# mLSTM's gates computed beside RWKV's first inverse, small gates in one pass, the early branch over two PSUM banks

## The chip, the cores and the metric

The kernel runs on one core of a Trainium2 chip. The core has a matrix engine (TensorE, PE), a vector engine (VectorE, DVE), a scalar engine (ScalarE, ACT), a general engine (GpSimd, POOL) and SyncE (SP), whose queue issues nearly all of the DMAs of this kernel. [...] The metric is device time in microseconds, the median of several executions; lower is better.

## The reference

Four layers over 512 tokens (256 context, 256 latent), 1024 channels. Each layer:

```python
hx = modulate(rmsnorm(x, norm1_g[l]), mod_x[0], mod_x[1])      # and hc for the context
gdn_x, rwkv_x, mlstm_x, gate_x = split_cols(hx @ w_in[l], col_groups)
a = gdn_branch(...); b = rwkv_branch(...); m = mlstm_branch(...)   # two directions each
merged = sum(sigmoid(gates[i]) * (branches[i] @ w_branch[i]) for i in range(3))
x = x + mod_x[2] * (merged @ w_out[l])
x = x + mod_x[5] * moe_ec(modulate(rmsnorm(x, norm2_g[l]), ...), ...)
```

The change touches the gates of mLSTM. Its scan keeps a running maximum per head and direction, from an input gate and the cumulated log of a forget gate:

```python
b = cumsum(log_sigmoid(fg + f_bias));  m_t = maximum(b_t + m, max_j(b_t - b_j + ig_j))
P = qk * exp(D - m_t);  num = exp(b + m - m_t) * (q @ C) + P @ v;  C = dec * C + wk.T @ v
```

These two gates of four heads and two directions, with gdn's eight decays and eight write strengths, come from 32 small columns of `w_in` ("small gates").

## The kernel before

Activations lie transposed, channels on partitions and the 512 tokens along the free axis, so a product with a block of 128 output channels fills one PSUM bank. Large products are exact to nearly fp32 by a split of both sides into a high and a low half of the one-pass type `fp32r`: three products for each 128 channels of depth (`dense`, L399 to L418). `load_w` (L387) loads raw weights four blocks of depth at a time into a buffer with the tag "raw" + f, casts them into "hi" + f on ScalarE and subtracts into "lo" + f on GpSimd (`split`, L383 to L385). f is "m" or "f"; each of these tags has two buffers, and the product goes to the bank "d" + f, of which there is one each ("dm", "df").

The kernel is written as streams of work. A planner orders each engine's instructions by a priority, a due time that the streams set with `at(t)` or `due(t, pace)` in units that are meant as microseconds of the layer; it gives buffers of one tag to the tiles that ask for them. Before a layer's clock starts at 0, `hh` and `hl`, the halves of the normed and modulated input, are made (L569 to L578). Then run, beside each other:
- `small_gates` (L653): 32 columns of small gates, as 16 fp32 matmuls in four column groups of 32 (two depths times `hh`, `hl`), copied, transposed and added up from four parts; softplus and the like follow, and `gdec`, `beta`, `igt` (input gate of mLSTM), `spf` (softplus of its forget gate).
- RWKV (streams "ai", "ac"): eight heads as four pairs. `rwkv_inputs` makes the inputs of a pair with `w_in` products of form "m", due from 40 us for pair 1; `rwkv_units` prepares two units in the tiles "AR" (three buffers), "BK" (one) and "t1" (five); `rwkv_pair` inverts triangular blocks (`tri_inverse`, L426: a substitution in 28 short VectorE steps between two trips through DRAM, then products; its tile `Zt` has the tag "BK") and runs the steps of the scan.
- gdn (stream "bi"): four heads, `w_in` products also of form "m", due from 95 us for head 1. In the program, gdn's heads 0 and 1 stand ahead of RWKV's pair 1.
- the fillers (L580 to L593): 36 `w_in` products of form "f" for the branch gates and mLSTM's q, k, v, spread over the layer, each copied out of "df" by ScalarE and stored in DRAM (`gates`). In the last layer they need only the latent half.
- mLSTM (L1279), due from 650, in the space that RWKV leaves: it loads q, k, v, transposes v and k, and then computes the gates: two padded tiles of gate columns, 16 matmuls for a transposed copy and a cumulated sum, three scans for the running maximum (L1342 to L1344), three exponentials, 16 transposes back to tokens into `tkm`, one product for the decays `dec`; the maximum goes to DRAM (`Md`) and comes back broadcast over partitions. The masked exponentials per head (L1399 to L1403), products and states follow.
- `first_branch` (L517), at 800: RWKV's output times `w_branch`, eight blocks of 128 channels. For each, `gated` (L510) loads the branch gate into `th`, multiplies (12 matmuls, bank "df"), forms (1 + th) times the product in VectorE (L515), and the result is stored in `part`. `th` has the tag "rawm".
- `second_branch` (L531), at 1500, loads gdn's output through tiles "him" and "lom" and splits it; `other_branches` (L539) does mLSTM's and gdn's products for the eight blocks, forms "f" and "m", and adds `part`. Then `w_out` and the expert mixture, which the change doesn't touch.

## Time and profile before

| | us |
|---|---|
| median of 3 runs | 4950.55 (4945.63 to 4950.76) |
| profiled execution | 4935.1 |
| its span, first to last instruction | 4933.3 |
| TensorE busy | 4447.4 (90%), 31792 matmuls |
| VectorE busy | 2927.6 (59%) |
| ScalarE, GpSimd busy | 1526.7 (31%), 1416.8 (29%) |
| granted TensorE clock, mean share of full speed | 0.954 |

The span holds four layers, which begin at about 43, 1303, 2553 and 3807 us; the last is shorter, since it needs only the latent tokens. The page gives sums over the whole span; what one stage waits for is read from views of a stretch: a table of busy times by stretch, the timeline, the waits of one engine or of the DMA queue, and the groups of instructions by line.

### The profile page before, as it was taken

Reading aid. Unit: us, or ns where it says so; the run is one execution under the profiler, and the core shown is the slowest. Engines: PE = TensorE matmul, PEld = TensorE weight load, DVE = VectorE, ACT = ScalarE, POOL = GpSimd, SP = SyncE. Lnnn points to the kernel's source line nnn. Section 1 sums busy time; section 2 is a strip of 40 time slices with the busy share of each in tenths; the row PEclk is TensorE's granted clock in tenths of the full one; section 3 lists DMA queues with packets and bytes.
Section 4 is the critical chain, followed back from the end, with each engine's and each line's share of the span. In section 5 each row is a group of like instructions: output and inputs, shape, how many; then the busy total and the mean of one; then the engine's idle time right before and its main releaser. Section 6 shows DMA issues by size and latency. Waiting matters only on the chain. (4 is left out here: it accounts for less than half of the span.)

```text
span 4933.3 us, 84704 instructions
## 1 busy us (share of the span) xinstructions
PE 4447.4 (90%) x31792; PEld 2903.0 (59%) x31792; DVE 2927.6 (59%) x8016; ACT 1526.7 (31%) x3100; POOL 1416.8 (29%) x1826
## 2 busy tenths in 40 slices
PE   7999999999889999989988999998998898887798
PEld 4666666653466666665336666666633666766532
DVE  4786767532477776663247777756423777767312
ACT  4343323221333332323124333332312433322211
POOL 3332323420243232242024323233301433332400
PEclk9999999999999999999999999999999899988899
DMA  6433446679632434457973244345698223333698
GB/s 228 118 111 109 123 150 202 230 268 386 238 105 66 124 113 125 152 190 265 386 282 112 66 115 118 111 146 167 243 382 300 88 78 85 88 87 108 222 386 310
DMA packets 716777, 886.01 MB, mean 180 GB/s; under 512 B 337072, under 2 KB 361264, under 8 KB 703568
## 3 DMA queue, kind: packets, MB, share of 16 engines
q1 hardware_dynamic: 716368, 880.60, 54.0%
q8 instruction: 251, 4.11, 0.3%
q14 instruction: 158, 1.29, 0.1%
HBM read 795.81 MB, written 84.63 MB: 178 GB/s over the span
## 5 line engine op out<-in xcount | busy, mean ns | idle before, releaser
L385 POOL TENSOR_TENSOR wlo<-wraw,whi 128x512 fp32r<-128x512 f32 x696 | 938.1, 1352 | 1725.8 <-ACT whi L384 1493.8
L411 PE MATMUL df<-big,whi 128*128 128x512 f32 (+1 forms) x2944 | 884.8, 382 | 0.0
L411 PE MATMUL dm<-big,whi 128*128 128x512 f32 (+1 forms) x2368 | 735.3, 390 | 0.0
L411 PE MATMUL df<-big,wlo 128*128 128x512 f32 (+1 forms) x1536 | 645.9, 420 | 65.9 <-ACT gt L590 21.4
L384 ACT CAST whi<-wraw 128x512 fp32r<-128x512 f32 x696 | 426.1, 617 | 886.3 <-PE df L411 446.8
L411 PEld LDWEIGHTS df<-big,whi 128*128 128x128 f32 x2944 | 562.4, 199 | 89.8 <-issue 3.8
L411 PE MATMUL dm<-big,wlo 128*128 128x512 f32 (+1 forms) x1248 | 524.8, 421 | 60.2 <-POOL wlo L385 17.4
L411 PEld LDWEIGHTS dm<-big,whi 128*128 128x128 f32 x2368 | 456.3, 197 | 80.1 <-issue 1.6
L411 PEld LDWEIGHTS df<-big,wlo 128*128 128x128 f32 x1536 | 303.9, 198 | 188.1 <-issue 102.0
L411 PEld LDWEIGHTS dm<-big,wlo 128*128 128x128 f32 x1248 | 245.5, 197 | 163.3 <-issue 57.6
L1686 PE MATMUL df<-mw,big 128*64 128x512 f32 x1024 | 282.8, 604 | 3.7 <-DMA mw<-in_w_dram 3.6
L1062 DVE SCALAR_TENSOR_TENSOR cv<-cv,par,cv 128x255 f32<-128x255 f32 (+3 forms) x472 | 253.8, 548 | 46.5 <-ACT cv L1059 42.6
L1686 PE MATMUL dm<-mw,big 128*64 128x512 f32 x1024 | 259.3, 596 | 5.6 <-DMA mw<-in_w_dram 5.6
L747 DVE SCALAR_TENSOR_TENSOR big<-cv,muc,big 128x252 f32<-128x252 f32 (+2 forms) x280 | 162.3, 603 | 40.8 <-ACT big L744 39.5
L1728 DVE SCALAR_TENSOR_TENSOR t<-t,df 128x512 f32<-128x512 f32 x32 | 22.0, 687 | 274.1 <-ACT t L1727 274.1
L1686 PEld LDWEIGHTS dm<-mw,big 128*64 128x64 f32 x1024 | 81.0, 137 | 164.5 <-issue 128.2
L385 POOL TENSOR_TENSOR mlof<-mrawm,mhif 128x512 fp32r<-128x512 f32 x9 | 11.6, 1284 | 540.3 <-ACT mhif L384 540.3
L212 PE MATMUL ai<-AR,BK 64*128 64x128 f32 (+1 forms) x1024 | 119.2, 313 | 44.8 <-POOL BK L930 21.7
L1745 PE MATMUL bi<-mw,mrawf 128*64 128x512 f32 x512 | 154.5, 601 | 0.3 <-DMA mw<-in_w_dram 0.3
L1686 PEld LDWEIGHTS df<-mw,big 128*64 128x64 f32 x1024 | 73.3, 136 | 131.4 <-issue 96.1
L1730 DVE TENSOR_TENSOR t<-t,dm 128x512 f32<-128x512 f32 x32 | 22.0, 687 | 193.6 <-PE dm L1686 193.6
L212 PEld LDWEIGHTS ai<-AR,BK 64*128 64x128 f32 x1024 | 91.2, 201 | 72.3 <-issue 30.3
(557 smaller groups left out, 7936.0 us busy)
## 6 DMA issues: line engine op xcount, KB each, us to landing
mw<-in_w_dram SPq DMA_DIRECT2D x768, 512.0 KB, 10.8
wraw<-in_w_in_dram SPq DMA_DIRECT2D x536, 256.0 KB, 2.8
adaw<-in_ada_w_dram SPq DMA_DIRECT2D x96, 1024.0 KB, 5.2
gates<-gt SPq DMA_DIRECT2D x114, 256.0 KB, 2.7
wraw<-in_w_branch_dram SPq DMA_DIRECT2D x96, 256.0 KB, 2.8
t<-gates SPq DMA_DIRECT2D x85, 256.0 KB, 4.3
TU<-zoai SPq DMA_DIRECT2D x128, 128.0 KB, 3.8
wraw<-in_w_out_dram SPq DMA_DIRECT2D x64, 256.0 KB, 4.2
```

The costliest lines, as they stand in the source:

```text
L212: mm(o, a, b, **kw)
L384: se.copy(dst_hi, src)
L385: eng.tensor_tensor(dst_lo, src, dst_hi.bitcast(F32), ALU.subtract)
L411: mm(ps[:, c0:c1], a[:, k % 4, :], bk[:, c0:c1], start=(n == 0), stop=(n == 3 * nk - 1))
L747: ve.scalar_tensor_tensor(dst, src, muc[:, 1 + q, rb:rb + 1], dst, ALU.mult, ALU.add)
L1062: ve.scalar_tensor_tensor(dst, src, cw[:, cb, t:t + 1], dst, ALU.mult, ALU.add)
L1686: mm(ps[64 * q:64 * q + 64, :], xe[k // 4][:, k % 4, e0 + q, :], wt[q][:, k2 * 512:(k2 + 1) * 512], start=(k == 0), stop=(k == 7))
L1728: ve.scalar_tensor_tensor(th, th, 1.0, ab[0], ALU.add, ALU.mult)
L1730: ve.tensor_tensor(hid, th, ab[1], ALU.mult)
L1745: mm(py[hf][64 * q:64 * q + 64, :], hT[:, kk, 64 * q:64 * q + 64], wt[q][:, kk % 2 * 512:kk % 2 * 512 + 512], start=(kk == 0), stop=(kk == 3))
```

## The change

Three edits. The early branch's blocks alternate between forms "f" and "m". The small gates take the split weights (`wq`: 32 high columns beside 32 low ones, in gdn's tile "Kt") in 16 one-pass matmuls with `hh` and `hl`, so two parts are added in place of four. mLSTM's gates leave `mlstm` for a function of their own, `mlstm_gates`, called behind the first two units of RWKV, with due time 20; it works in RWKV's tiles "BK", "AR" and "t1" and in the bank "ac", joins the two banks of the 16 matmuls into one, and hands `tkm` and `dec` on through DRAM (`tkd`), from where `mlstm` loads them.

```diff
+T_MG = 20.0
...
-                gated(1, db, (ab[:, 0], ab[:, 1]), th, "f")
+                gated(1, db, (ab[:, 0], ab[:, 1]), th, "fm"[db % 2])
...
                 rwkv_units(zr, l, 0, P, R, pair, S, last, oc)
+                MG = mlstm_gates(zr, G)
                 pair.append(rwkv_inputs(zr, l, 1, P, R, w_in, oc))
...
-                mlstm(zm, l, P, G, gates, oc, T_M, first_branch)
+                mlstm(zm, l, P, MG, gates, oc, T_M, first_branch)
...
         sy.dma_start(wsr, A["w_sm"][l])
+
+        wq = z.mt([4, 128], "Kt").bitcast(F32R).rearrange("p a (b w) -> p (a b) w", b=2)
+        split(wq[:, :, 0:32], wq[:, :, 32:64], wsr)
         pss = z.psm()
-        for k in range(0, 8, 2):
-            for q in range(4):
-                h = (hh, hl)[q // 2].bitcast(F32)
-                z.mm(pss[32 * q:32 * q + 32, :], wsr[:, k + q % 2, :], h[:, k + q % 2, :], start=(k == 0), stop=(k == 6), tile_position=(0, 32 * q))
+        for k in range(8):
+            for h in (hh, hl):
+                z.mm(pss[0:64, :], wq[:, k, :], h[:, k, :], start=(k == 0 and h is hh), stop=(k == 7 and h is hl))
...
         ve.tensor_copy(sm, ptv[:, :, 0])
-        for q in (1, 2, 3):
-            ve.tensor_tensor(sm, sm, ptv[:, :, q], ALU.add)
+        ve.tensor_tensor(sm, sm, ptv[:, :, 1], ALU.add)
...
+    def mlstm_gates(z, G):
+
+        z.due(T_MG, 0.0)
+        tiles = TILES
+        bk, ar_ = z.mt([2, 512], "BK"), z.mt([2, 512], "AR", 3)
+        ar, nb, M, ev_ = bk[:, 0], bk[:, 1], ar_[:, 0], ar_[:, 1]
+        igp, spp = z.mt([256], "t1", T1), z.mt([256], "t1", T1)
+        sm = z.mt([256], "t1", T1)
...
+        tkd = dp.tile([128, 144], F32, tag="tkd", name=nm("tkd"))
...
+        ps = z.psc()
+        for i, (o, src) in enumerate(((igp, G["igt"]), (spp, G["spf"]))):
...
+        sy.dma_start(tkd, sm[:, 0:144])
+        return dict(Md=Md, tkd=tkd)
+
+    def mlstm(z, l, P, MG, gates, oc, t, meanwhile):
...
+        tkd = z.mt([144], "mtk")
+        sy.dma_start(tkd, MG["tkd"])
```

The steps inside `mlstm_gates` that are left out here (scans, exponentials, transposes back, decays) are those of `mlstm` before, in the other tiles.

## Rows read from the trace of the kernel before

**Rows 1.** The page, busy time of each engine.
```profile
PE 4447.4 (90%) x31792; PEld 2903.0 (59%) x31792; DVE 2927.6 (59%) x8016; ACT 1526.7 (31%) x3100; POOL 1416.8 (29%) x1826
```

**Rows 2.** Busy us by stretch: length, each engine (instructions), clock, DMA share, GB/s.
```profile
782.00:880.00 98.00, 92.72 (x582) 66.57 (x580) 81.59 (x253) 30.55 (x61) 29.85 (x28) 1.00 0.57 193
...
1340.00:1470.00 130.00, 116.39 (x755) 87.10 (x755) 94.73 (x225) 52.69 (x105) 57.15 (x73) 0.95 0.37 109
...
2033.00:2131.00 98.00, 88.27 (x518) 64.64 (x516) 81.24 (x248) 30.21 (x59) 28.88 (x28) 0.98 0.39 124
2137.00:2170.00 33.00, 26.56 (x129) 19.66 (x127) 15.93 (x27) 9.90 (x17) 11.80 (x11) 1.00 0.67 219
2172.00:2219.00 47.00, 44.92 (x192) 34.88 (x190) 33.19 (x39) 14.72 (x26) 24.32 (x17) 1.00 0.71 228
...
4488.00:4563.00 75.00, 56.45 (x347) 43.08 (x344) 59.91 (x198) 18.20 (x44) 16.00 (x18) 0.75 0.32 99
```

**Rows 3.** Timeline of the early branch, layer 1: start, us, engine, line, operation.
```profile
2141.30 0.69 DVE L515 SCALAR_TENSOR_TENSOR mg<-mg,df 128x512 f32<-128x512 f32 x1 [0.21 <-PE df L411]
...
2144.16 0.42 SPq L512 DMA_DIRECT2D mg<-gates  x1
...
2145.14 0.69 DVE L515 SCALAR_TENSOR_TENSOR mg<-mg,df 128x512 f32<-128x512 f32 x1 [0.15 <-PE df L411]
...
2145.97 0.47 PE L411 MATMUL df<-big,wlo 128*128 128x512 f32 x1 [0.87 <-DVE mg L515]
```

**Rows 4.** SP queue's waits, 2137 to 2170: us in total, times, longest.
```profile
SPq L512 <- DMA part<-mg: 7.4, 5, 2.4
```

**Rows 5.** SP queue's waits, 1800 to 1850.
```profile
SPq L512 <- POOL wlo L385: 8.5, 2, 4.9
```

**Rows 6.** ScalarE's timeline: copies of `w_in` products, gdn's (L1058), RWKV's (L743).
```profile
1481.34 0.58 ACT L1058 COPY cv<-dm 128x512 f32<-128x512 f32 x1 [3.50 <-PE dm L411]
...
1505.57 0.59 ACT L743 COPY cv<-dm 128x512 f32<-128x512 f32 x1 [4.67 <-PE dm L411]
```

**Rows 7.** DMA issues, 2137 to 2170: KB each, median us to landing.
```profile
wraw<-in_w_branch_dram SPq DMA_DIRECT2D x9, 256.0 KB, 2.7
part<-mg SPq DMA_DIRECT2D x8, 256.0 KB, 2.5
mg<-gates SPq DMA_DIRECT2D x7, 256.0 KB, 3.3
```

**Rows 8.** Groups by line, 2137 to 2170: count, busy us, mean ns, idle before.
```profile
L385 POOL TENSOR_TENSOR wlo<-wraw,whi 128x512 fp32r<-128x512 f32 x9 | 12.4, 1381 | 26.9 <-ACT whi L384 26.9
...
L384 ACT CAST whi<-wraw 128x512 fp32r<-128x512 f32 x9 | 5.6, 617 | 28.1 <-PE df L411 28.1
```

**Rows 9.** Groups by line of mLSTM's gates, 2033 to 2056, TensorE and VectorE.
```profile
L212 PE MATMUL ai<-cst,mC 128*32 128x128 f32 x32 | 2.9, 279 | 0.0
L1342 DVE TENSOR_TENSOR_SCAN mM<-t,mar 32x512 f32<-32x512 f32 x1 | 2.2, 2170 | 0.0
...
L216 PE MATMUL ai<-cst,mar 64*128 64x64 f32 x4 | 0.4, 221 | 0.0
...
L1376 DVE TENSOR_TENSOR mdg<-mel,cst 64x32 f32<-64x32 f32 x1 | 0.2, 173 | 0.0
```

**Rows 10.** ScalarE's timeline, last layer: first and last copy of mLSTM's gates.
```profile
4493.28 0.58 ACT L1323 COPY t<-ai 64x512 f32<-64x512 f32 x1 [2.74 <-PE ai L212]
...
4510.98 0.21 ACT L1383 COPY mtk<-ai 128x64 f32<-128x64 f32 x1 [0.78 <-PE ai L216]
```

**Rows 11.** Groups by line, TensorE, 1300 to 1330: the small gates' matmuls.
```profile
L212 PE MATMUL bi<-big,TU 128*32 128x512 f32 x32 | 8.4, 664 | 0.8 <-DVE big L574 0.8
```

**Rows 12.** Start of layer 1: timeline of the small weights' load, and its landing.
```profile
1300.05 0.33 SPq L662 DMA_DIRECT2D TU<-in_w_sm_dram  x1
...
1302.83 1.27 DVE L569 SCALAR_TENSOR_TENSOR t<-big,der,adm 128x256 f32<-128x256 f32 x3 [1.18 <-ACT adm L380]
...
TU<-in_w_sm_dram SPq DMA_DIRECT2D x1, 128.0 KB, 5.4
```

More of the change, by code (lines that the diff above doesn't have):

```diff
@@ L1281, in mlstm @@
+    def mlstm(z, l, P, MG, gates, oc, t, meanwhile):
+        tiles = TILES
         z.due(t - OFF, P_M * PS)
@@ L1305, in mlstm @@
         H = z.mt([4, 4, 128], "mH")
-        Md = dp.tile([2, 4, 512], F32, tag="Md", name=nm("Md"))
         qkd = dp.tile([4, 128, 4, 128], F32, tag="qkd", name=nm("qkd"))
         tl = oc // 128
-        rw = slice(0, 64)
-        igp, spp = z.mt([4, 2, 32], "mC", 2), z.mt([4, 2, 32], "mC", 2)
-        for o, src in ((igp, igt), (spp, spf)):
-            gp.memset(o, 0.0)
-            ve.tensor_copy(o[:, :, :, 0:4], src.rearrange("p t (d h) -> p t d h", d=2))
-        pig, pnb = z.psm(), z.psm()
@@ L1316, in mlstm @@
-        for t in range(4):
-            ts_ = slice(t * 128, (t + 1) * 128)
-            for d in range(2):
-                dr = slice(32 * d, 32 * d + 32)
-                z.mm(pig[dr, ts_], igp[:, t, d, :], ident, start=True, stop=True, tile_position=(0, 32 * d))
-                z.mm(pnb[dr, ts_], spp[:, t, d, :], C[f"mf_{d}"], start=True, stop=True, tile_position=(0, 32 * d))
-        ar, nb = z.mt([512], "mar"), z.mt([512], "t2")
-        se.copy(nb[rw], pnb[rw])
-        ve.tensor_tensor(ar[rw], pig[rw], nb[rw], ALU.add)
@@ L1325, in mlstm @@
-        d0 = z.mt([512], "t2")
-        gp.memset(d0[rw], 0.0)
-        tiles = [[0, 1, 2, 3], [1, 0, 3, 2]]
-        def ent(d, t):
-            return t * 128 + 127 * d
-        def ext(d, t):
-            return t * 128 + 127 * (1 - d)
-        mpv = z.mt([4], "mpv")
-        gp.memset(mpv[rw], 0.0)
-        M = z.mt([512], "mM")
-        r0, r1 = slice(0, 32), slice(32, 64)
-        for d, dr in enumerate((r0, r1)):
-            for q in range(1, 4):
-                e, x = ent(d, tiles[d][q]), ext(d, tiles[d][q - 1])
-                ve.tensor_scalar(d0[dr, e:e + 1], nb[dr, x:x + 1], -1.0, None, ALU.mult)
@@ L1342, in mlstm @@
-        ve.tensor_tensor_scan(M[r0], d0[r0], ar[r0], 0.0, ALU.add, ALU.max)
-        ve.tensor_tensor_scan(M[r1, 0:256][:, ::-1], d0[r1, 0:256][:, ::-1], ar[r1, 0:256][:, ::-1], 0.0, ALU.add, ALU.max)
-        ve.tensor_tensor_scan(M[r1, 256:512][:, ::-1], d0[r1, 256:512][:, ::-1], ar[r1, 256:512][:, ::-1], M[r1, 0:1], ALU.add, ALU.max)
-        for d, dr in enumerate((r0, r1)):
-            sy.dma_start(Md[d], M[32 * d:32 * d + 4])
-            for q in range(1, 4):
-                t, x = tiles[d][q], ext(d, tiles[d][q - 1])
-                ve.tensor_tensor(mpv[dr, t:t + 1], M[dr, x:x + 1], nb[dr, x:x + 1], ALU.subtract)
@@ L1350, in mlstm @@
-        Mv = M[rw].rearrange("p (t w) -> p t w", t=4)
-        arv = ar[rw].rearrange("p (t w) -> p t w", t=4)
-        tkm = z.mt([4, 4, 2, 4], "mtk")
-        dg = z.mt([2, 4, 4], "mdg")
-        dec = z.mt([2, 4, 2], "mdec")
-        for q in range(4):
-            src = ar
-            if q:
-                src = z.mt([512], "t2")
-                ev = src[rw].rearrange("p (t w) -> p t w", t=4)
-            if q == 1:
-                ve.tensor_tensor(ev, mpv[rw, :, None].to_broadcast([64, 4, 128]), Mv, ALU.subtract)
-            elif q == 2:
-                ve.tensor_tensor(src[rw], nb[rw], M[rw], ALU.subtract)
-            elif q == 3:
-                for d, dr in enumerate((r0, r1)):
-                    ve.tensor_tensor(ev[dr], arv[dr], Mv[dr, :, ext(d, 0):ext(d, 0) + 1].to_broadcast([32, 4, 128]), ALU.subtract)
-            if q:
-                se.activation(src[rw], src[rw], AF.Exp)
-            if q == 1:
-                el = z.mt([4], "mel")
-                for d, dr in enumerate((r0, r1)):
-                    ve.tensor_copy(el[dr], ev[dr, :, ext(d, 0)])
-                sel = ident[rw, 0:64].rearrange("p (d x) -> p d x", d=2)[:, :, 0:4]
-                ve.tensor_tensor(dg[rw], el[rw, None, :, None].to_broadcast([64, 2, 4, 4]), sel[:, :, None, :].to_broadcast([64, 2, 4, 4]), ALU.mult)
-            if q % 2 == 0:
-                ptk = z.psm()
-            for t in range(4):
-                o = q % 2 * 256 + t * 64
-                z.tr(ptk[:, o:o + 64], src[rw, t * 128:(t + 1) * 128], ident[rw, rw])
-            if q % 2:
-                se.copy(tkm[:, q - 1:q + 1].rearrange("p q t d h -> p (q t) d h"),
-                        ptk.rearrange("p (q d x) -> p q d x", q=8, d=2)[:, :, :, 0:4])
@@ L1385, in mlstm @@
-        pdc = z.psm()
-        z.mm(pdc[:, 0:32], C["ones"][rw, :], dg[rw].rearrange("p d a b -> p (d a b)"), start=True, stop=True)
-        pdv = pdc[:, 0:32].rearrange("p (a b q) -> p a b q", a=8, b=2)
-        for p in range(2):
-            hp = slice(64 * p, 64 * p + 64)
-            ve.tensor_copy(dec[hp].rearrange("p d t b -> p (d t) b"), pdv[hp, :, :, p])
+        Md = MG["Md"]
+        tkd = z.mt([144], "mtk")
+        sy.dma_start(tkd, MG["tkd"])
+        tkm = tkd[:, 0:128].rearrange("p (k t d h) -> p k t d h", k=4, t=4, d=2)
@@ L1391, in mlstm @@
+        dec = tkd[:, 128:144].rearrange("p (d t b) -> p d t b", d=2, t=4)
         ss = z.mt([4, 4], "mss")
```

72 lines of the change are left out of this document (68 added, 4 removed).

## Prediction

> **What bounds the kernel now.** I read the page first: TensorE is at work through 90% of the span [rows 1], so a change pays only where TensorE stands still or where its work shrinks. Then I cut one layer into stages with the table of stretches [rows 2]. In the stretch that mLSTM shares with gdn's last head (2033 to 2131 in layer 1) TensorE works 88.27 of 98 us and VectorE 81.24: both are close to full, so work taken out of it shortens it. In the early branch (2137 to 2170) TensorE works only 26.56 of 33 us and VectorE half the time: that stage waits. In the stage behind it (2172 to 2219) 192 matmuls take 44.92 us, 0.234 us each, and nothing waits; 12 of them, one block of a branch product, take 2.8 us, and a block comes every 2.94 us (47 over 16). Third, the timeline inside the early branch [rows 3]: the evacuations start 3.84 us apart, and the first matmul of the next block starts 0.14 us after the evacuation of the last has ended, its idle time ended by that evacuation. So there it is the one PSUM bank that paces. Fourth, the DMA queue's own waits, which tell who shares buffers [rows 4, 5].
>
> **Part 1, the early branch over two banks.** What it is meant to remove: 3.84 - 2.94 = 0.9 us for each of 8 blocks, 7 us in each of layers 0 to 2.
>
> What it adds is not in the diff's line. An odd block now takes form "m", and with it the raw weights' buffers "rawm", two in number. The block's gate tile `th` also lies in "rawm". The trace shows that they are the same buffers: the first gate tiles of the branch, at 1820, waited for the low-half subtraction of a `w_in` weight (two waits, 4.9 us the longest) [rows 5]. It shows the order in which such buffers are given out, too: RWKV's inputs of pair 1, due from 40 us, were evacuated (1505.57) after those of gdn's head 1, due from 95 us (1481.34), which stand ahead of them in the program [rows 6]. So program order counts within one set of buffers, not due time. For "rawm" this order becomes th0, th1, w1, th2, th3, w3, and so on, in two buffers. A gate tile gives its buffer up when its product has landed in `part`; already the waits of before show that (`mg<-gates` behind `part<-mg`, 5 times) [rows 4].
>
> I follow one cycle from the issue of an odd block's weights: landing 2.7 us [rows 7], cast 0.62, subtraction 1.38 [rows 8], 12 matmuls 2.8, evacuation 0.69 [rows 3], store landed 2.5 [rows 7]: 10.7 us, and with some 0.12 us at each of five handovers 11.3. Meanwhile the next even gate tile takes the buffer that the weights left after 4.7 us: load 3.3, evacuation 0.69, store 2.5, 11.2 us, with handovers 11.6. Both must end before the next odd weights can be loaded, so a pair of blocks takes about 11.6 us in place of 7.7. The first odd weights start when block 0's store has landed (2.5 us after the first evacuation, which doesn't move); three cycles and the last block's 7.5 us later the branch is done: 2.5 + 34.8 + 7.5 = 45 us, against 7 x 3.84 + 3 = 30 now. Behind it, the stage that adds the other branches needs "rawm" again for its first odd weights, 0.9 + 2.5 + 4.8 = 8 us later, and finds 2 of its 16 blocks (5.9 us) done while TensorE waited. Net 15 + 8 - 6 = 17 us, less the 3 us by which that stage trails the branch's end today: **+13 us in each of layers 0 to 2** (14, rounded down since the order of release may favour one cycle), +39. Bounds: with a store that gives its buffer up as early as in rows 3 (the gate load there is issued 2.17 us after an evacuation's end, handover included) and no other handovers, 10.4 a pair, +9 a layer, and +8 with the two cycles in step; with a TensorE at its lower level after each wait, +18 (rival C). `second_branch`'s loads, next in program order for "him" and "lom", now come behind the branch's last odd weights; at 2.7 + 2 us [rows 7, 8] they are ready before those of the next stage and cost nothing beside it; without that cover, 2 us.
>
> The Trainium skill (DMA: Bandwidth & Descriptors, "Latency and other measured facts") puts most of the fixed cost of a DMA, about 2 us, into the round trip to the memory, and says that a lighter load shortens it. By an estimate with 2 us for each landing the cycle would be 10.1 us and the branch's loss 8 us a layer; the rows say 2.5 to 3.3 [rows 7] at 219 GB/s [rows 2].
>
> **Part 2, mLSTM's gates beside the first inverse.** Removed from mLSTM's stage: TensorE work of 5.2 us (four groups, first and last in [rows 9]) and VectorE work of 10.2 us (twelve groups, likewise [rows 9]) in a layer, and a chain that takes 18 us in the last layer, from 4493.28 to 4511.2 [rows 10]. What comes in its place, one load of 72 KB (128 x 144) from DRAM, is issued behind V's loads, hundreds of us after its data were stored, and is hidden; were it late, 2.7 us.
> - Layer 1: VectorE is at 83%, TensorE at 90% [rows 2]. The 98 us hold 88 of TensorE; less 5 that is 83, and at the 95% that layer 0 reaches (92.72 of 98) the stretch takes 87: -11; I take -10, since the fillers there still share one bank, and the same for layer 2.
> - Layer 0 is at 95% now: only TensorE's 5.2 us and a little go: -6.
> - Layer 3 has no fillers left; TensorE works 56.45 of 75 us [rows 2] and the chain counts: up to -14. But the early branch runs inside that stretch, and with half-size transfers of about the same landing its four pairs take as long as in Part 1, while its steps stand behind mLSTM's. I take -4 for both (bounds -14 and +6).
> - What it costs where it goes: the rows `BK` become free after the second unit, so the chain falls into the 1408 to 1460 of layer 1, beside the 28 short VectorE steps of the inverse. The stretch 1340 to 1470 has 13.6 us of idle TensorE and 35 of idle VectorE in 130 [rows 2], room for 5 and 10 us, but these run in order: a scan of 1.2 us ahead of an inverse step holds it. I take +3 a layer (bounds 0 and 8). SP gets three stores more beside the inverse's own; at 0.4 us of issue each (as in rows 3) they are inside the 3. `BK`'s next user, the inverse's off-diagonal product, comes only behind all those steps and their trip through DRAM.
>
> Sum -26 - 4 + 9 (the +3 of layer 3 is inside its -4): **-21**.
>
> **Part 3, small gates in one pass.** 32 records, 8.4 us of busy TensorE in a layer [rows 11], become 16 of 0.234: 3.7. But TensorE waits there for the normed input, so I count 2 of the 4.7 us. VectorE loses two additions and gains one subtraction. Against it: the weights now need a split, and in layer 1 they landed 5.4 us after 1300.05, while VectorE begins the normed input at 1302.83 [rows 12]. If the subtraction stands ahead of that in VectorE's order, it holds it for 2.6 us. **-1 a layer, -4** (bounds -4 and +3 a layer).
>
> **Sum.** +39 - 21 - 4 = +14 us on the profiled execution's 4935.1 us: 4949. The median of the runs shown is 15 us above that execution, 4950.55, so I predict 4950.6 + 13.4 = **4964 us**.
>
> **Rivals.**
> - *A, the banks alternate as meant.* It needs the gate tiles and the odd weights not to hold each other up: -7 in three layers in place of +13, and 6 more from layer 3's stage. -21 - 6 - 21 - 4 = -52: 4898. For it: the paced bank is plain in rows 3. Against: rows 4 and 5. The Trainium skill (Perfetto Trace Analysis, "Optimization Strategy") says that a gap repeating on the engine that should be full can mean too few SBUF or PSUM buffers; by that rule a second bank is the cure, and the rows agree on the gap, but it names SBUF as well. 13%.
> - *B, the wait is short and the gates pay in full.* +8 a layer, no cost beside the inverse: 24 - 26 - 10 - 8 = -20: 4930. 17%.
> - *C, slower by much.* TensorE runs at its lower level (1.2 of 2.4 GHz) in the odd blocks, because each follows a wait: 12 matmuls then take up to twice 2.8 us. For it: in layer 3's stretch, a quarter of it idle, the granted clock is 0.75; against: it is 1.00 in the early branch now [rows 2]. That lies in the chain of every pair, +2 four times, so +18 to +21 a layer; with inverse steps held by 5 us more in each layer that is +60 - 21 + 20 - 4 = +55: 5006. It decides once the wait ahead of an odd block lets the granted clock fall. 13%.
> - *D, the gates move but mLSTM's stage doesn't shrink*, since the fillers' bank and not VectorE paces it: +39 + 3 - 4 = +38: 4989. 9%.
> - The forecast: 48%; its own range is 4942 to 4986.
>
> **How the numbers follow.** I call 0.2% (10 us) what a measurement of this kernel can tell from no change. Faster by more is A, most of B: 27%. Within it is the lower half of the forecast's range and the rest of B: 22%. Slower is the rest: 51%. The range 4910 to 5004 leaves out A's centre and C's centre, some 10% on each side.
>
> **What would show it.** In the profile after: in layers 0 to 2 the waits of the DMA queue would show `wraw<-in_w_branch` behind `part<-mg` in the early branch, the evacuations would pair up with 11 to 12 us from one odd one to the next, and TensorE would idle there some 15 us more a layer. The evacuation would no longer be what ends TensorE's idle time. mLSTM's first masked exponentials would come some 15 us earlier after gdn's head 3, and the scans would stand beside the inverse. The chain from the normed input to the first `cv<-dm` would be 1 to 2 us shorter, or longer if the split holds it. The prediction is wrong if odd weights are loaded before block 0's store has landed, or if the stage of other branches starts within 3 us of where it starts now.

## The result, and the profile after

| | before | after |
|---|---|---|
| median of the runs, us | 4948.1 (4943.5 to 4950.8) | 5060.3 (5042.6 to 5064.3) |
| ratio, 95% interval | | 1.0228 (1.0212 to 1.0243) |
| span of the profiled execution, us | 4933.3 | 5057.4 |
| layers 0 to 3, from one normed input to the next (the last to the end of the span), us | 1259.9, 1250.6, 1253.3, 1126.6 | 1311.6, 1280.6, 1286.5, 1135.0 |

The change makes the kernel 2.3% slower: 112 us by the medians, where 14 were forecast. The direction was right, by Part 1 alone, since Parts 2 and 3 came out with the other sign; the size is far outside the range. The layers are 52, 30, 33 and 8 us longer. These lengths come from one execution each, before's 13 us below its median, so they add up to 123. In layer 0 the delay is there before the branch: gdn's last step ends 28 us later, against 9 and 12 us in layers 1 and 2.

The page of the changed kernel, the line that answers to [rows 1] and one group (busy, mean ns, idle before it and what ended most of that):

```profile
PE 4496.2 (89%) x31728; PEld 2939.9 (58%) x31728; DVE 2923.2 (58%) x8012; ACT 1528.7 (30%) x3104; POOL 1429.9 (28%) x1826
...
L412 PE MATMUL dm<-big,wlo 128*128 128x512 f32 (+1 forms) x1312 | 568.1, 433 | 162.1 <-POOL wlo L386 96.7
```

TensorE has 64 matmuls fewer and is busy 49 us longer. Products into the bank "dm" wait 96.7 us for GpSimd's low halves (`wlo`).

Busy us by stretch, columns as in [rows 2], at the same distances from each layer's start (for mLSTM's stage of layer 1 within 1.5 us): mLSTM's stage in layer 0, the first inverse and mLSTM's stage in layer 1, then layer 1's early branch (58 us now), the stage behind it, and the last layer's mLSTM stage.

```profile
782.80:880.80 98.00, 95.91 (x601) 64.41 (x600) 77.75 (x238) 28.42 (x56) 30.93 (x30) 1.00 0.61 209
...
1392.50:1522.50 130.00, 116.04 (x671) 86.38 (x673) 96.59 (x251) 52.51 (x106) 58.96 (x84) 0.91 0.37 109
2084.00:2182.00 98.00, 90.74 (x539) 67.48 (x538) 79.67 (x246) 28.35 (x55) 29.57 (x27) 0.98 0.41 135
...
2192.00:2250.00 58.00, 34.60 (x120) 25.68 (x120) 11.65 (x19) 7.78 (x13) 12.04 (x11) 0.74 0.46 145
2252.00:2302.00 50.00, 45.45 (x189) 35.26 (x188) 31.22 (x40) 15.19 (x26) 22.99 (x17) 0.97 0.65 208
...
4603.70:4678.70 75.00, 55.30 (x336) 42.75 (x336) 55.13 (x187) 14.65 (x34) 16.98 (x20) 0.73 0.34 99
```

The early branch stands out: 120 matmuls in 58 us at a granted clock of 0.74, against 129 in 33 us at 1.00 [rows 2]. Beside the first inverse TensorE is as busy as before but gets through 671 instructions in place of 755, at 0.91 against 0.95. mLSTM's stages have no less of TensorE in them at the same place: 95.91 of 98 us in layer 0 (92.72 before), 90.74 in layer 1 (88.27), 55.30 of 75 in the last layer, at 0.73 (56.45 at 0.75). The stage behind the branch runs at 0.97 where it stood at 1.00.

The timeline of one pair of blocks there (as in [rows 3]):

```profile
2192.10 0.69 DVE L516 SCALAR_TENSOR_TENSOR mg<-mg,df 128x512 f32<-128x512 f32 x1 [3.80 <-PE df L412]
...
2194.16 1.00 SPq L393 DMA_DIRECT2D wraw<-in_w_branch_dram  x2
...
2198.52 1.35 POOL L386 TENSOR_TENSOR wlo<-wraw,whi 128x512 fp32r<-128x512 f32 x1
2199.90 0.32 SPq L513 DMA_DIRECT2D mg<-gates  x1
...
2199.93 0.79 PE L412 MATMUL dm<-big,wlo 128*128 128x512 f32 x1 [4.01 <-POOL wlo L386]
...
2205.38 0.69 DVE L516 SCALAR_TENSOR_TENSOR mg<-mg,dm 128x512 f32<-128x512 f32 x1 [5.36 <-PE dm L412]
2205.99 0.68 DVE L516 SCALAR_TENSOR_TENSOR mg<-mg,df 128x512 f32<-128x512 f32 x1
2206.10 0.92 SPq L530 DMA_DIRECT2D part<-mg  x2
...
2208.79 3.34 SPq L393 DMA_DIRECT2D wraw<-in_w_branch_dram  x2
```

The first odd weights are issued only once the first gate tile has been stored (second of the two issues at 2194.16), their low half is ready at 2199.87, and the 12 matmuls then take until 2205.38, 5.45 us where a block took 2.8 before. The even block just ahead of that wait still ran at the full clock, the odd block behind it at half of it (columns as in [rows 2]):

```profile
2192.90:2195.60 2.70, 2.67 (x12) 2.17 (x12) 1.80 (x2) 0.43 (x1) 1.23 (x1) 1.00 0.35 124
2199.93:2205.10 5.17, 5.17 (x12) 3.79 (x12) 0.09 (x1) 0.00 (x0) 0.00 (x0) 0.50 0.60 196
```

The second odd block takes longer still, 8.1 us from 2213.71. Eleven matmuls of an even block stand between its own, since both blocks have one due time and the planner then takes their matmuls in turn:

```profile
2219.59 0.39 PE L412 MATMUL dm<-big,whi 128*128 128x512 f32 x1
2219.82 0.40 PE L412 MATMUL df<-big,whi 128*128 128x512 f32 x1
...
2221.84 0.69 DVE L516 SCALAR_TENSOR_TENSOR mg<-mg,dm 128x512 f32<-128x512 f32 x1 [4.79 <-PE dm L412]
```

The buffer that the first odd weights left takes the next gate tile 0.03 us after the subtraction (2199.90), and the next odd weights wait for that tile's store (2208.79). The last evacuation of the branch starts at 2249.53, 57.4 us behind its first; before (second row) that was at 2165.33, 27.9 us behind the first one at 2137.42.

```profile
2249.53 0.69 DVE L516 SCALAR_TENSOR_TENSOR mg<-mg,dm 128x512 f32<-128x512 f32 x1 [1.49 <-DMA mg<-br]
```

```profile
2165.33 0.69 DVE L515 SCALAR_TENSOR_TENSOR mg<-mg,df 128x512 f32<-128x512 f32 x1 [3.17 <-PE df L411]
```

The waits of the DMA queue and of TensorE in the branch (2190 to 2255 and 2192 to 2250: us in total, times, longest) show the chain whole: stores that wait for evacuations hold the loads behind them in the queue, and TensorE waits for low halves.

```profile
SPq L530 <- DVE mg L516: 20.3, 7, 4.9
SPq L393 <- POOL wlo L386: 8.1, 5, 2.6
SPq L513 <- POOL wlo L386: 6.3, 4, 2.0
SPq L393 <- DMA part<-mg: 5.5, 5, 2.1
```

```profile
PE dm L412 <- POOL wlo L386: 21.6, 4, 9.3
```

### The profile page after: what moved, and what is told of

Read it like the earlier page. It is cut to its first block, busy times and chain, and to the rows that moved or that the text cites. A ratio compares the mean times of both kernels' runs of the same rounds, so it can differ in the third digit from the quotient of the medians.

```text
span 5057.4 us, 84622 instructions
## 1 busy us (share of the span) xinstructions
PE 4496.2 (89%) x31728; PEld 2939.9 (58%) x31728; DVE 2923.2 (58%) x8012; ACT 1528.7 (30%) x3104; POOL 1429.9 (28%) x1826
## 5 line engine op out<-in xcount | busy, mean ns | idle before, releaser
L412 PE MATMUL df<-big,whi 128*128 128x512 f32 (+1 forms) x2816 | 851.9, 383 | 0.0
L412 PE MATMUL dm<-big,whi 128*128 128x512 f32 (+1 forms) x2496 | 803.2, 401 | 7.0 <-DVE big L575 6.6
L412 PE MATMUL dm<-big,wlo 128*128 128x512 f32 (+1 forms) x1312 | 568.1, 433 | 162.1 <-POOL wlo L386 96.7
L412 PE MATMUL df<-big,wlo 128*128 128x512 f32 (+1 forms) x1472 | 621.7, 422 | 55.9 <-ACT gt L591 20.0
L412 PEld LDWEIGHTS df<-big,whi 128*128 128x128 f32 x2816 | 540.0, 200 | 86.7 <-issue 3.4
L412 PEld LDWEIGHTS dm<-big,whi 128*128 128x128 f32 x2496 | 498.2, 204 | 103.8 <-DVE big L575 11.6
L412 PEld LDWEIGHTS dm<-big,wlo 128*128 128x128 f32 x1312 | 266.2, 203 | 271.4 <-POOL wlo L386 111.3
L412 PEld LDWEIGHTS df<-big,wlo 128*128 128x128 f32 x1472 | 291.4, 198 | 178.8 <-issue 69.2
L1065 DVE SCALAR_TENSOR_TENSOR cv<-cv,par,cv 128x255 f32<-128x255 f32 (+3 forms) x472 | 234.4, 505 | 27.1 <-ACT cv L1062 23.1
L448 DVE TENSOR_TENSOR Y<-Y,sv 128x14 f32<-128x14 f32 (+8 forms) x448 | 125.8, 284 | 6.8
```

The lines of the kernel that those rows point to most:

```text
L412: mm(ps[:, c0:c1], a[:, k % 4, :], bk[:, c0:c1], start=(n == 0), stop=(n == 3 * nk - 1))
L448: ve.tensor_tensor(Xb[:, j + 1:, 0:j], Xb[:, j + 1:, 0:j], tv, ALU.add)
L1065: ve.scalar_tensor_tensor(dst, src, cw[:, cb, t:t + 1], dst, ALU.mult, ALU.add)
```

## Experiments

Each difference below is against the median of the kernel before on the same chip in the same group of runs (4947 to 4954 us). The ratio and its interval use all runs of the group, so they can differ from that difference by some us. Theory 1: the buffers that gate tiles and odd weights share carry most of the loss. Theory 2: the moved gates hold RWKV's chain, and mLSTM's stage doesn't give it back. Theory 3: it is the small gates, which come later. The rivals of each stand in the expectations.

### The three parts one by one

The early branch alone:

```diff
-                gated(1, db, (ab[:, 0], ab[:, 1]), th, "f")
+                gated(1, db, (ab[:, 0], ab[:, 1]), th, "fm"[db % 2])
```

> The kernel before with the early branch alone changed (odd blocks in form m: weights, their halves and the bank). Theory 1, the buffers that gate tiles and odd weights share set the pace and carry most of the loss: in the trace of the changed kernel the branch's stretch grew by 19, 25 and 25 us in layers 0 to 2 and the stage behind it by some 3 us each, so this alone gives 4948 + 75 = about 5023 us, and its branch takes 55 to 60 us a layer. Rival, the loss comes from the gates' work beside the inverse and the branch is only late by what stands ahead of it: 4948 + 10 to 40, 4958 to 4988 us, and its branch takes under 45 us.

Measured: 5037.8 us, ratio 1.0167 (1.0150 to 1.0185), +88. The branch takes 58 us in each of layers 0 to 2 (before 28 in layer 1), and its stretch in layer 1 shows the same picture as the changed kernel's:

```profile
2169.30:2226.00 56.70, 33.73 (x126) 25.20 (x125) 12.35 (x23) 9.13 (x15) 12.04 (x11) 0.76 0.41 136
```

mLSTM's gates alone (`mlstm_gates` behind `rwkv_units`, branch all in form f, small gates as before):

> The kernel before with mLSTM's gates alone moved beside the first inverse (early branch all in form f, small gates as before). Theory of the prediction: 4948 - 21 = 4927 us. Theory 2, the gates' steps hold RWKV's chain and mLSTM's stage does not give it back, as the changed kernel's trace has it (RWKV's and gdn's steps end 9 to 28 us later in each layer, the early branch's first evacuation 2 to 28 us later): 4948 + 30 to 48, so 4978 to 4996 us, with gdn's last steps 9 us or more later than before in layers 1 and 2. Theory 3, it is the small gates that delay the chain and this move is harmless: 4920 to 4945 us.

Measured: 4951.4 us, 1.0000 (0.9990 to 1.0011), +1: neither the gain of the prediction nor the loss of theory 2. But the zero is a sum. The lengths below come from one execution each, before's 15 us below its median, so they add up to +15 where the medians show +1; which layer carries these 15 us no trace shows. Whole layers, before (layers 1 and 3) and with the gates moved (layers 1 and 3), columns as in [rows 2]:

```profile
1302.80:2553.40 1250.60, 1155.66 (x8090) 745.89 (x8090) 761.10 (x2064) 391.10 (x783) 358.29 (x456) 0.97 0.54 180
...
3806.70:4933.30 1126.60, 949.24 (x7302) 654.63 (x7302) 653.06 (x1802) 340.58 (x729) 333.28 (x449) 0.90 0.49 160
```

```profile
3843.50:4948.90 1105.40, 935.04 (x7302) 644.51 (x7302) 645.09 (x1802) 342.15 (x729) 334.20 (x449) 0.93 0.51 163
1311.30:2579.20 1267.90, 1170.77 (x8090) 758.20 (x8090) 750.62 (x2063) 389.68 (x783) 366.22 (x456) 0.95 0.55 177
```

Layers 0, 1 and 2 are 8, 17 and 11 us longer, the last is 21 shorter. In layer 1 the same 8090 matmul records take 15.1 us more of TensorE at a mean clock of 0.95 instead of 0.97: that is nearly all of its 17 us. In the last layer it is the other way: 14 us less of TensorE, at 0.93 instead of 0.90.

The small gates alone (weights split by `split(wq[:, :, 0:32], wq[:, :, 32:64], wsr)`, 16 products, branch and mLSTM as before):

> The kernel before with the small gates' products alone in the one-pass form. Theory of the prediction: 4948 - 4 = 4944 us. Theory 3, the small gates come later (their copy 4 to 7 us later and their first exponential 6 to 9 us later in each layer of the changed kernel) and that delays RWKV and gdn: 4948 + 20 to 45, so 4968 to 4993 us. Theory 2 (the moved gates carry the delay): within 10 us of 4948, although the copy is 4 us late here too, since the first shifted input comes 5 us earlier.

Measured: 4959.1 us, 1.0013 (1.0003 to 1.0024), +9. Start of layer 1 in that run: the last normed row, the split's subtraction, the first of the 16 products, the copy of their sum:

```profile
1316.38 2.65 DVE L574 SCALAR_TENSOR_TENSOR big<-t,mod,big 128x256 fp32r<-128x256 f32 x2 [0.20 <-ACT big L571]
...
1318.95 0.41 DVE L385 TENSOR_TENSOR Kt<-TU,Kt 128x256 fp32r<-128x256 f32 x1
...
1319.51 1.57 PE L212 MATMUL bi<-big,Kt 128*64 128x512 f32 x6
...
1324.84 0.58 ACT L671 COPY t<-bi 64x512 f32<-64x512 f32 x1
```

The subtraction stands behind the last normed row in VectorE's order, so none of the 16 products starts before 1319.5, 15.2 us into the layer; before, 30 of the 32 [rows 11] had run by then, each as its rows came. The copy comes at 20.6 instead of 16.7 us, the exponential of gdn's decays (`eg`) at 40.3 instead of 34. By the interval the loss is 2 to 12 us.

The other two parts together, without the branch:

> The changed kernel with the early branch back in form f, so only the moved gates and the one-pass small gates are left. If the three parts add up: 4950 + 1 + 6 = 4957 us, and then the branch costs 100 us beside the other two where it costs 88 alone. If the gates and the small gates hinder each other (both delay gdn's decays and the first inverse): 4975 us or more.

Measured: 4975.8 us, 1.0053 (1.0034 to 1.0071), +26, where the two alone give 10. So of the 112 us the branch is 86 to 88, and some 26 are the other two, which hinder each other.

### What makes the branch long

The banks alternate and nothing else (a `bank` argument for `gated`; weights and buffers of form f):

```diff
-            pb = psum("d" + f)
+            pb = psum("d" + (bank or f))
```

> The kernel before with the early branch's blocks alternating between the two PSUM banks alone; weights, halves and gate tiles keep the buffers that they have before (form f), so gate tiles and odd weights no longer meet. Theory 1: the evacuations come 2.9 to 3.3 us apart instead of 3.84, the branch takes 25 to 28 us instead of 32.5, and 4948 - 10 to - 20 gives 4928 to 4938 us. Rival, the block's pace is set by its weights' way through the two buffers of form f (load, cast, subtraction) and the bank's wait only stands in front of it: no change, 4943 to 4953 us, the evacuations 3.8 us apart again. Rival, a second bank in use makes the stage of the other branches or the fillers wait for it: 4955 us or more.

Measured: 4969.1 us, 1.0037 (1.0022 to 1.0053), +19. My first theory fell: free banks alone make it slower. (PSUM is the memory that TensorE writes its products to; a bank holds one product of 128x512, and it has to be evacuated, read out by VectorE or ScalarE, before the next block can use it. Gate tiles and weights lie in SBUF, the other on-chip memory.) Two matmuls of the branch in layer 1, then evacuations, the last of them by the stage behind:

```profile
2144.78 0.39 PE L411 MATMUL dm<-big,wlo 128*128 128x512 f32 x1
2145.01 0.39 PE L411 MATMUL df<-big,whi 128*128 128x512 f32 x1
...
2145.89 0.69 DVE L515 SCALAR_TENSOR_TENSOR mg<-mg,df 128x512 f32<-128x512 f32 x1 [4.17 <-PE df L411]
...
2146.50 0.68 DVE L515 SCALAR_TENSOR_TENSOR mg<-mg,dm 128x512 f32<-128x512 f32 x1
...
2154.07 0.69 DVE L515 SCALAR_TENSOR_TENSOR mg<-mg,df 128x512 f32<-128x512 f32 x1 [1.36 <-PE df L411]
...
2163.14 0.69 DVE L515 SCALAR_TENSOR_TENSOR mg<-mg,df 128x512 f32<-128x512 f32 x1 [4.53 <-DMA mg<-gates]
...
2179.80 0.69 DVE L515 SCALAR_TENSOR_TENSOR mg<-mg,df 128x512 f32<-128x512 f32 x1 [5.45 <-DMA mg<-gates]
```

Two blocks come full together, 0.6 us apart, every 8.2 to 9 us, and later ones wait for the gate tile's load. All eight blocks have one due time (`at(AM0 + AMS * db)` with AMS = 0), so the planner alternates the matmuls of two blocks one by one. That is why nothing is gained: the branch takes 27.8 us from its first evacuation to its last, as before (27.9). The loss lies behind it. From there to the end of the next stage it is 56.8 us in place of 50.8 (4 to 5 us more in layers 0 and 2): that stage's first gate tile lies in "rawm" too, and its evacuation waits for the tile's load (2179.80). So the time came out where the last rival had it, behind a wait for gate tiles; that wait holds the next stage more than the branch.

Two forms as in the change, but the gate tiles in two buffers of their own in mLSTM's pool:

```diff
-                th = w2k("rawm")
+                th = zm.mt([512], "thb", 2)
```

> The early branch over two forms, as in the changed kernel, but its gate tiles in two buffers of their own in mLSTM's pool instead of sharing rawm with the odd weights; all else as in the kernel before. Theory 1, the sharing is what makes the branch 58 us long: the branch falls to about 35 us, where the banks alone stand, and the time to 4960 to 4972 us. Rival, the odd blocks are long because TensorE works at its lower clock in them (12 matmuls in 5.3 us instead of 2.8) and because part's stores hold the loads behind them in SP's order: the branch stays over 48 us and the time over 5005 us.

Measured: 4937.6 us, 0.9974 (0.9963 to 0.9985), -12. One tag changed, 100 us gone: theory 1 holds for the branch, and the rival's causes (clock, order of stores) are consequences of the shared buffers. The first odd block of layer 1 is evacuated 95 us ahead of the others (95 to 103 us in layers 0 to 2), since its weights wait for nobody now; the other seven follow within 24 us, at a granted clock of 0.93:

```profile
2045.83 0.69 DVE L515 SCALAR_TENSOR_TENSOR thb<-thb,dm 128x512 f32<-128x512 f32 x1
...
2141.04 0.69 DVE L515 SCALAR_TENSOR_TENSOR thb<-thb,df 128x512 f32<-128x512 f32 x1 [1.69 <-PE df L411]
...
2164.65 0.69 DVE L515 SCALAR_TENSOR_TENSOR thb<-thb,dm 128x512 f32<-128x512 f32 x1
```

That may be why the result is better than expected; no run tests it.

Banks alone with four gate tiles (`zm.mt([512], "thb", 4)`):

> The banks alternate alone (weights all in form f), and the gate tiles have four buffers of their own instead of two of rawm. Theory: with two banks it was the gate tile's way (store, load, evacuation, 2 buffers) that set 8.2 us for a pair of blocks; with four the pair takes 5.9 to 6.5 us, the branch 24 to 28 us, the stage behind it no longer waits for a first tile, and the time is 4930 to 4942 us. Rival, the pair is set by the weights' way through two buffers of form f (load 2.7, cast 0.62, subtraction 1.3, twice through one queue), 8 us: no change against the banks alone, 4962 to 4975 us.

Measured: 4946.3 us, 0.9994 (0.9981 to 1.0006), -3. The tiles were worth 22 us, but a pair still takes 8.2 us or more and the branch 26 to 29: a miss. No load is waited for any more, the stage behind is back at 48 to 51 us, and the two blocks still come full together:

```profile
2137.91 0.69 DVE L515 SCALAR_TENSOR_TENSOR thb<-thb,df 128x512 f32<-128x512 f32 x1 [3.99 <-PE df L411]
...
2138.51 0.68 DVE L515 SCALAR_TENSOR_TENSOR thb<-thb,dm 128x512 f32<-128x512 f32 x1
...
2146.09 0.69 DVE L515 SCALAR_TENSOR_TENSOR thb<-thb,df 128x512 f32<-128x512 f32 x1 [0.27 <-PE df L411]
```

The same with the blocks due one after the other:

```diff
-AM0, AMS = 800.0, 0.0
+AM0, AMS = 800.0, 0.1
```

> As the run with two banks and four gate tiles, but the blocks have due times 0.1 us apart instead of one and the same. There the matmuls of two blocks alternated one by one, so both banks came full together and TensorE waited for both evacuations, 7.7 us a pair as with one bank. Theory: one block after the other lets the one bank be evacuated while the other fills: 5.9 to 6.6 us a pair, the branch's eight evacuations within 21 to 25 us, time 4922 to 4938 us. Rival, the weights' way through the two buffers of form f sets the pair: 7.5 us or more and 4942 to 4950 us.

Measured: 4918.2 us, 0.9935 (0.9912 to 0.9959), -29. In layer 1 the evacuations come 2.7 us apart, from bank to bank (about as close in layer 0, unevenly in layer 2), and TensorE stands full at clock 1.00 (evacuations, then the stretch 2128 to 2148):

```profile
2130.74 0.69 DVE L515 SCALAR_TENSOR_TENSOR thb<-thb,dm 128x512 f32<-128x512 f32 x1 [1.63 <-PE dm L411]
2133.47 0.69 DVE L515 SCALAR_TENSOR_TENSOR thb<-thb,df 128x512 f32<-128x512 f32 x1 [2.03 <-PE df L411]
2136.19 0.69 DVE L515 SCALAR_TENSOR_TENSOR thb<-thb,dm 128x512 f32<-128x512 f32 x1 [2.03 <-PE dm L411]
...
2128.00:2148.00 20.00, 19.65 (x87) 15.71 (x86) 5.58 (x9) 4.38 (x8) 9.00 (x7) 1.00 0.74 223
```

The bank was the bound, as [rows 3] said, but a second bank alone lost 19 us. With gate tiles that nobody else holds it brought 3, which is no clear change, and with the blocks in turn as well 29. Whether the turn would pay without the tiles, or without the second bank, no run shows. The Trainium skill (Perfetto Trace Analysis, "Optimizing Tensor Performance") says that independent groups of matmuls should rotate through the banks, so that the evacuation of one overlaps the matmuls of the next. The last run is that rule at work; the runs with the banks alone and with four tiles rotate as well and gain nothing, since two groups in lockstep have no next one.

The changed kernel itself with two gate tiles of its own:

> The changed kernel as it is, but the early branch's gate tiles in two buffers of their own in mLSTM's pool. Theory 1: sharing rawm is the whole of the branch's loss, here as in the kernel before, where the same edit took 5038 to 4938 us: 4976 (all in f) - 12 = 4964 us, 4955 to 4972, and the branch's evacuations within 28 us. Rival, the branch in the changed kernel is also held by what the moved gates leave late: 4985 us or more.

Measured: 4984.4 us, 1.0064 (1.0041 to 1.0087), -76 against the changed kernel. The sharing is most of the branch's loss here too, but it is 20 us above the expected sum, and 8 above the same kernel with the branch in form f, which the two intervals can't tell from nothing. So beside the moved gates two forms bring no gain even with tiles of their own. The branch itself is as short as with own tiles alone (24 us from the second evacuation to the last in layer 1, in both); what is lost is lost outside it, and why is open.

### What the gates and the small gates cost

The small gates alone, with their weights split in the middle of the normed input:

```diff
                 for k in range(8):
+                    if k == 4:
+                        wq_ = small_weights(zg, l)
```

> The kernel before with the one-pass small gates (alone: 4959 us), but their weights are split in the middle of the normed input instead of behind it. In the trace of the run with the split behind it, all 16 products wait for the split's subtraction, which VectorE reaches only after its last normed row; the copy of the result came 4 us and the first exponential 6 us later than before. Theory: the lateness is the split's place; with it early the copy comes at 15 to 17 us after the layer's start and the exponential by 35, and the time is 4942 to 4952 us. Rival, the 6 us more come from the one-pass form's own place in TensorE's order: copy at 19 us or later, 4955 us or more.

Measured: 4943.0 us, 0.9998 (0.9986 to 1.0011), -4. The copy of the products comes at 15.8 us, the exponential of gdn's decays at 31.7 in layers 1 and 2. So the split's place made the small gates late, and with it the loss goes; that -4 is a gain is not shown (-7 to +5).

The same edit with the gates moved (all but the branch):

> The changed kernel with the early branch in form f (4976 us) and the small gates' split in the middle of the normed input. The moved gates alone cost 1 us and the small gates alone 9, together 26. Theory 3: the late small gates push the moved gates' chain, which hangs on them, further into the inverse; with the split early the two cost what the moved gates cost alone: 4946 to 4956 us, with the first scan of the last layer at 114 us instead of 117 and its first off-diagonal product at 152 instead of 160. Rival, both fill the same idle stretches of VectorE and TensorE before the inverse, whatever their order: 4966 us or more.

Measured: 4956.0 us, 1.0009 (0.9995 to 1.0022), +9 in place of +26 (by the ratio -2 to +11). The last layer's first scan comes at 112.2 us instead of 117.5 and its first off-diagonal product at 154.5 instead of 160.5. So some 17 of the 26 us were the late small gates: mLSTM's gates hang on them and were pushed further into the inverse.

The gates moved not beside the first inverse but behind gdn's first head, due at 200 (small gates and branch as before):

```diff
-T_MG = 20.0
+T_MG = 200.0
...
-                MG = mlstm_gates(zr, G)
                 pair.append(rwkv_inputs(zr, l, 1, P, R, w_in, oc))
                 rwkv(0)
                 gdn(0)
+                MG = mlstm_gates(zr, G)
```

> The kernel before with mLSTM's gates moved (alone, due 20 us: 4951 us), but behind gdn's first head in the program and due 200 us, so beside RWKV's second pair instead of the first inverse. With the gates beside the first inverse, layers 0 to 2 were 8 to 17 us longer and the last 21 shorter. Theory 2, the cost is the place, the inverse's short steps that stand in VectorE's order behind scans and reductions: here the first off-diagonal product is back at 152 to 153 us, layers 0 to 2 cost under 5 us each or gain, and the time is 4915 to 4938 us. Rival, any extra work in the fore part lengthens it by about what mLSTM's stage saves, for TensorE is the bound there and its clock falls with each new gap: 4942 to 4958 us.

Measured: 4983.6 us, 1.0070 (1.0050 to 1.0090), +36: worse than beside the inverse, so the theory of the place falls: the first off-diagonal product of the inverse comes about when it came before (153.5 and 151.2 us into layers 1 and 2, 152.8 and 153.4 before), and the kernel is slower all the same. Layers 1 and 2 are 8 and 5 us longer than before (17 and 11 with the early place), but layers 0 and 3 are 19 us longer each. What holds layers 0 and 3 here was not settled.

The gates moved in the last layer alone:

```diff
-                mlstm(zm, l, P, G, gates, oc, T_M, first_branch)
+                if last:
+                    mlstm_late(zm, l, P, MG, gates, oc, T_M, first_branch)
+                else:
+                    mlstm(zm, l, P, G, gates, oc, T_M, first_branch)
```

> mLSTM's gates moved beside the first inverse in the last layer alone; layers 0 to 2, the early branch and the small gates as in the kernel before. With the gates moved in every layer, the last layer was 1105 us long instead of 1127 and the others 8 to 17 us longer. Theory, the move pays where no fillers are left and mLSTM's chain counts, and costs where the inverse is already close to full: 4950 - 20 = 4926 to 4936 us. Rival, the last layer's gain hangs on what the layers before leave behind, or a whole layer's time shifts by some 10 us with any new order: 4943 to 4957 us.

Measured: 4925.8 us, 0.9953 (0.9937 to 0.9969), -24. The last layer's first masked exponential comes 37 us earlier (668.6 instead of 706), RWKV's last steps end 11 us earlier, and the layer takes 1108.9 us instead of 1126.6 (columns as in [rows 2]). The move pays in the layer where no filler is left:

```profile
3811.10:4920.00 1108.90, 934.64 (x7302) 643.75 (x7302) 643.17 (x1802) 342.01 (x729) 334.65 (x449) 0.93 0.51 163
```

### Versions that put the findings together

Two forms with own gate tiles, and the gates of the last layer; then the same with due times 0.1 us apart:

> Two forms with gate tiles of their own (alone: 4938 us) and mLSTM's gates moved in the last layer alone (alone: 4926 us); small gates as before. If both gains add: 4950 - 12 - 24 = 4914 us, 4907 to 4921. If the last layer's gain is the same room that the branch uses there: 4922 to 4932 us.

> As the run before it (two forms, own gate tiles, gates moved in the last layer), with the branch's blocks due 0.1 us apart. Theory of the lockstep: pairs of 6 to 6.6 us instead of about 7.9, some 4 to 6 us in each of layers 0 to 2: 4895 to 4904 us. Rival, with two forms the blocks no longer run in lockstep and the gate tile's way through two buffers sets the pair: within 6 us of the run before it.

Measured: 4916.0 us (0.9928, 0.9905 to 0.9951) and 4914.9 us (0.9934, 0.9913 to 0.9956). The two gains add. Due times in turn bring nothing with two forms: there the second expectation's rival was right.

Banks in turn in form f, four gate tiles, and the gates of the last layer:

> Banks in turn in form f with four gate tiles (alone: 4918 us, -29) and mLSTM's gates moved in the last layer alone (alone: 4926 us, -24); small gates as before. If the two add: 4895 to 4900 us. If the last layer gains from both by the same room (its branch runs inside mLSTM's stage): 4903 to 4912 us.

Measured: 4878.7 us, 0.9864 (0.9842 to 0.9885), -69, the best of all. The two parts alone gave -29 and -24; the 16 us beyond their sum are not clear of the three intervals.

The same with the repaired small gates, and then the whole change with all three faults mended:

> Banks in turn in form f with four gate tiles, mLSTM's gates moved in the last layer alone (together: 4879 us), and the one-pass small gates with their split in the middle of the normed input (alone: 4943 us, -4). If the last adds: 4872 to 4878 us. Rival, the last layer's gates again start later behind the one-pass small gates and lose there what the first three layers gain: 4879 to 4886 us.

> The changed kernel with all three of its parts, each with its fault mended: the branch alternates between the banks in form f with four gate tiles and due times 0.1 us apart, the small gates' split stands in the middle of the normed input, mLSTM's gates stay moved in every layer. If the parts add: 4956 - 29 = 4927 us, 4920 to 4934. If mLSTM's stage and the branch behind it gain more when the branch no longer waits (as the last layer showed: -69 where -53 were due): 4900 to 4918 us, near the 4898 us forecast for banks that alternate as meant. Rival, the moved gates' cost in layers 0 to 2 grows with it: 4936 us or more.

Measured: 4902.4 us (0.9902, 0.9873 to 0.9932) and 4922.1 us (0.9940, 0.9917 to 0.9962). The small gates don't pay beside the last layer's gates: 24 us go with them. That layer's first masked exponential comes at 681.0 instead of 669.8 and the layer is 7 us longer; the rest of the 24 is open. The last run differs from the one before only in that the gates of layers 0 to 2 are moved too, and 20 us more go with that. So the change as it was meant, mended, is 32 us faster than before (19 to 41 by the interval; its parts, -29 for the banks in turn and +9 for the rest, would give 20). Of its distance to the 4879 some 24 us lie in the small gates and 20 in the moved gates of layers 0 to 2.

## Why the prediction was wrong

**What bounds the kernel** was read rightly. The evacuation of the one bank paces the early branch; with banks in turn the step falls from 3.84 [rows 3] to 2.7 us, below the 2.94 that I took from [rows 2].

**Part 1, the mechanism: right.** The shared "rawm", the order of its buffers and the wait of `wraw<-in_w_branch` behind `part<-mg` are in the trace as forecast, and one tag undoes 100 us.

**Part 1, the size: wrong, +13 a layer forecast, 21 to 28 measured (24 to 31 with the branch alone).** From the branch's first evacuation to the end of the stage behind it layer 1 takes 107.1 us in place of 79.4. All of that, and 2 us more, is in the branch: 57.4 us from its first evacuation to its last, where I had 45, against 27.9 before. The first cycle by the timeline above: load 2.7, cast and subtraction 2.3, as forecast; matmuls 5.45 in place of 2.8; two evacuations in a row 1.3 in place of 0.7; store 2.1. That is 13.9 us against 11.6, and the three cycles between odd evacuations take 14.7 on average (2205.38 to 2249.53). The failed step is the term of 2.8 us for the 12 matmuls of an odd block, the price at the full clock. They took 5.45, 8.1, 5.1 and 5.5 us in layer 1, 13 us more in sum, which is what the branch is longer than the 45 forecast. By an estimate some 3 of them are the even block's matmuls in the second odd block, and the rest, some 10, is the clock. I forecast 15 us more of idle TensorE in the branch and kept its work at the price of the full clock, because the row of before said 1.00. With the idle time that I forecast myself (23 of 58 us stand idle now, 6 of 33 before) the granted clock is 0.74, and a matmul takes 0.288 us (34.60 over 120) in place of 0.206 (26.56 over 129): 10 us for 120 of them. Rival C had this, at +2 four times, as a case of 13%, and its condition came true: the odd blocks stand behind waits of 4.0, 3.4, 9.3 and 4.8 us, and the first of them ran at 0.50.

The stage behind, forecast at -1 net (8 late, 6 in advance, 3 of today's trail), takes 2 us less behind the branch's last evacuation (48.9 in place of 50.8): right.

**Part 2, forecast -21, measured +1.** In layers 0 to 2 I had -3, -7 and -7; in the profiled executions they are +8, +17 and +11 (all four layers add up to +15 there, and the medians say +1). The price at the inverse itself was near: its first off-diagonal product comes 6, 3 and 4 us later, 3 were forecast. Two steps failed. mLSTM's stage, from gdn's last step to the early branch's first evacuation, shrinks by 1, 4 and 5 us and not by 6, 10 and 10; that is nearest to rival D. In the whole change TensorE has as much to do at that place as before (90.74 of 98 us in layer 1, 88.27 before), so fillers are the likely reason, but no run tests it. And the delay grows on the way: gdn's steps end 11 to 14 us later. In layer 1 the rows show that as 15 us more of TensorE for the same matmuls, at a lower mean clock; whether the clock is the cause or follows from new gaps, no run separates. In the last layer I took -4 and it is -21 to -24: there I charged the branch's cycle against it, which the runs with the branch in form f don't have, and I didn't count that RWKV's own chain would end 11 us earlier (both by the run with the last layer's gates alone).

**Part 3, forecast -4, measured +9.** I had bounded only the case that the split's subtraction stands ahead of the normed input. It stands behind it, where VectorE is free but all 16 products wait. With the split in the middle it is -4 (-7 to +5).

**The sum.** I added three parts that are not independent: alone they are +88, +1 and +9, together 112. The small gates feed mLSTM's gates, and once these stand early, a late small gate is a late inverse: some 17 us, that is about 8 more than the small gates lose alone.

**The rivals.** A, the banks alternate as meant, gave 4898 for the whole change; mended, it measures 4922. C, 5006, was nearest and still 54 us short: its clock is there, but at about 10 us a layer on the forecast's 13, and of the held inverse steps 3 to 6 us show at the first off-diagonal product.

## What to carry to other kernels

Here a second PSUM bank paid once the gate tiles had buffers of their own and the blocks came in turn: look for the tag that two users share and for due times that are equal. When a forecast puts new waits ahead of matmuls (3.4 to 9.3 us here), carry the lower clock as a term with a price, since the rows of before, with waits of 0.9 us in this place, show only the full one. When work is moved ahead, look at what it hangs on. Price the parts of a change together where one feeds the other.

## What the runs showed of the hardware

The early branch ran at a granted clock of 1.00 with 6 us idle in 33, at 0.74 to 0.76 with 23 in 57 to 58, and at 1.00 again with 0.35 in 20. At the lower of TensorE's two levels (1.2 and 2.4 GHz; granted clock 0.50 behind a wait of 4.01 us) the first odd block's 12 matmuls took 5.45 us, twice the 2.7 to 2.8 at the higher; the others took 5.1 and 5.5, and 8.1 with eleven foreign matmuls between. A price for the odd blocks alone (2.65 us four times) would have been 10.6 us a layer, about what the branch's busy time shows (10 us); no bigger effect of the clock was needed. In the traces of before and after VectorE and ScalarE are the only engines that read PSUM banks; no row of GpSimd does.
